# Up product of a decoder layer: some low parts by accumulating loads, convolutions in pieces, and the last product's sums reloaded pair by pair

## The chip, the cores and the metric

The kernel runs on one core of one Trainium2 chip. The metric is the device time of one execution in microseconds (us); the time shown for a kernel is the median of its runs. The profile names the engines PE (TensorE's matmuls), PEld (its weight loads), DVE (VectorE), ACT (ScalarE), POOL (GpSimd) and SP (SyncE); SP and POOL issue nearly all the DMAs.

## The reference

One decoder layer on x of 256 tokens by 2048, all in float32. A wide input product feeds forgetting attention (8 heads), a matrix memory (mLSTM, 4 heads) and two gates; the two branches are projected, gated, added, multiplied by w_out and added to x. Then comes the feed-forward part, where the change works:

```python
        h2 = rmsnorm(x, norm2_g[l])
        u = causal_dwconv(jnp.einsum('bsd,df->bsf', h2, w_up[l]), conv_w[l], conv_b[l])
        u_gate, u_val = u[..., :D_FF], u[..., D_FF:]
        x = x + jnp.einsum('bsf,fd->bsd', jax.nn.silu(u_gate) * u_val, w_down[l])
```

causal_dwconv adds three taps over the tokens to each channel; D_FF is 5632. So w_up is 2048 x 11264 and w_down 5632 x 2048.

## The kernel before

**Products in parts.** Every product is made of three matmuls in the type fp32r: each operand is split into a high part (a copy rounded to fp32r) and a low part (the operand minus its high part), and high x low, high x high and low x high are added in PSUM (`prod`, L287). Activations are split by `put` (L195). Weights are split as they arrive: ACT writes the high part wh, DVE subtracts it from the raw weights and writes the low part wl (`split_sub`, L172 and L173).

**Weights.** They are stored as chunks of 128 x 2048 floats (1 MB), each cut into pieces (`add_chunk`, L100). SP loads chunks into a ring of three buffers raw (L135 to L137); wh and wl have rings of three. `next_sub` (L178) asks for the chunks up to two ahead, splits the coming pieces, and hands out the next.

**Blocks of the large products.** `s_block` (L280) makes 256 tokens x 1024 columns in one go, over pairs of 128 rows of the weights. A pair of kind p ("plain") takes two pieces and 8 x 3 = 24 matmuls of 128 x 512. A pair of kind S saves one product in eight by working with sums and differences of the weights (DVE makes them, L157 to L167, tile sums) and of the activations (`put_sums`): four pieces, 21 matmuls, four more PSUM tiles, and some additions afterwards. Strings such as UP_PAIRS give the kinds: the up product has 8 pairs a block, 2 of them S, in 11 blocks (up0 to up10); the last product (y0, y1) has 22 pairs a block, 8 of them S, in two blocks.

**Work between the pieces.** `tasks` is a list of closures; each piece of an s_block takes the next `per_piece` of them (`run_tasks`, L190). During block b of the up product they are the transposes of block b-1's result (`as_columns`, L933: PE, then ACT), its convolutions (`convolved`, L944: ACT, DVE, ACT, DVE) and the split of the outcome g (tile ghl) with, for some pairs, its sums. All engines take their instructions in the order in which this Python code issues them, as the scheduler has placed them.

**Memory.** The tag a8 is a ring of 15 buffers of 8 KB per partition. g has 22 pairs. The first N_OUT = 6 are sent to DRAM (g_dram, L978) and come back (gback, L1010) before the last product; the sums of the 8 S pairs go to s_dram (L975) and come back in three loads of 1 MB (s_ops, L1016). POOL issues these DMAs, and in its order they stand one behind the other.

**Start.** x, transposed, is loaded by SP in eight parts between the first chunks of weights; POOL builds the constants (identity matrices, masks, sel) and then, on the same queue, issues the two loads of x as rows (xt, L486).

Of the kernel before, what the change touches and what calls it, by code (L numbers as in the profile page):

```python
# [10 lines left out]
F32 = mybir.dt.float32  # L11
# [6 lines left out]
P = 128  # L18
# [34 lines left out]
C_G1, C_G2, C_QG, C_KG, C_MG, C_CONV = 0, 16, 32, 33, 34, 42  # L53
CST = C_CONV + 2 * NF * 4


# [11 lines left out]
def trunk(ctx: ExitStack, tc: tile.TileContext, a):  # L68
# [16 lines left out]
    def a8(name, shape, dtype=F32):  # L85
        return big.tile([P, *shape], dtype, tag="a8", bufs=15, name=name)

# [25 lines left out]
    def add_pairs(ap, patterns):  # L113
        for i, kind in enumerate("".join(patterns)):
            pieces = ("b", "b21", "t13", "t24") if kind == "S" else ("whole", "whole")
            add_chunk(ap[i], 2048, pieces)

# [7 lines left out]

    raws, subs, s_tiles = {}, {}, {}
    n_chunk = len(chunks)
# [11 lines left out]
    def split_sub(j):  # L139
# [9 lines left out]

        if kind == "whole":  # L150
            src = raw[:, s * n : (s + 1) * n]
# [20 lines left out]
        nc.scalar.activation(wh[:, :n], src, AF.Copy)  # L172
        nc.vector.tensor_tensor(wl[:, :n], src, wh[:, :n].bitcast(F32), ALU.subtract)  # L173
        subs[j] = (wh[:, :n], wl[:, :n])

    state = {"sub": 0}

    def next_sub(ahead=2):  # L178
        j = state["sub"]
        state["sub"] = j + 1  # L180
        i = subs_of[j][0]
        for c in range(i, i + 3):
            load_chunk(c)
        for q in range(j, j + ahead):
            split_sub(q)
        return subs.pop(j)
# [3 lines left out]
    def run_tasks(n):  # L190
        for _ in range(min(n, len(tasks))):
            tasks.pop(0)()

# [86 lines left out]
    def s_block(name, pairs, s_ops, pattern, pools, dst, add=True, per_piece=0):  # L280
# [22 lines left out]
        for m, kind in enumerate(pattern):  # L303
# [3 lines left out]

            if kind == "p":
# [79 lines left out]
    for _ in range(9):  # L388
# [5 lines left out]
    ident = const.tile([P, P], F32, name="ident")  # L394
    make_identity(nc, ident)
    identb = const.tile([P, P], BF16, name="identb")
    make_identity(nc, identb)
    upper = const.tile([P, P], F32, name="upper")
    make_upper_triangular(nc, upper)
    ones = const.tile([P, P], F32, name="ones")  # L400
    nc.gpsimd.memset(ones, 1.0)
    mhalf = const.tile([P, 8], F32, name="mhalf")
    nc.gpsimd.memset(mhalf, -0.5)
    mask_qk = const.tile([P, P], BF16, name="mask_qk")
    make_causal_mask(nc, mask_qk, mask_val=-BIG)
    mask_st = const.tile([P, P], BF16, name="mask_st")
    nc.gpsimd.memset(mask_st, 0.0)
    nc.gpsimd.affine_select(
        out=mask_st, in_=mask_st, compare_op=ALU.is_ge, fill=BIG, base=0, pattern=[[1, P]],
        channel_multiplier=-1,  # L410
    )


    sel = const.tile([3 * 32, FH, P], BF16, name="sel")
    nc.gpsimd.memset(sel, 0.0)
    for i in range(3):
        nc.gpsimd.affine_select(
            out=sel, in_=sel, compare_op=ALU.not_equal, fill=1.0, base=-32 * i,
            pattern=[[-1, FH], [0, P]], channel_multiplier=1,
        )  # L420
    nFT = const.tile([3 * 32, S], BF16, name="nFT")
    MT = const.tile([3 * 32, S], BF16, name="MT")
    nc.gpsimd.memset(MT, 0.0)

# [53 lines left out]
    for k in range(KD):  # L478
# [4 lines left out]
        product_b(z, hT, k, [wh[:, c] for c in cols], [wl[:, c] for c in cols], k == 0, k == KD - 1)  # L483
        if k == 2:
            for tok in range(2):
                nc.gpsimd.dma_start(xt[tok], a["x"][tok * P : (tok + 1) * P, :])  # L486
        if k >= KD // 2:
# [73 lines left out]

    qT, kT, fv = a8("qT", [FH, S]), a8("kT", [FH, S]), a8("fv", [2, FOXW])
    mqkT = a8("mqkT", [2, MH, S])
# [10 lines left out]
    def qk_evac(z, dst, b, gcol, scale, name):  # L574
        for tok in range(2):
# [16 lines left out]
            def finish(tok=tok, qn=qn):  # L592
                ps = transpose4(qn, f"ps_{name}{b}{tok}")
                g = cst[:, gcol : gcol + 1]
                out = dst[:, 4 * b : 4 * b + 4, tok * P : (tok + 1) * P]
                nc.vector.tensor_scalar(out, ps, g, scale, ALU.mult, ALU.mult)
# [3 lines left out]
    for b in range(2):  # L600
        qk_evac(block_b(f"fq{b}", hT, KD, 512), qT, b, C_QG, FD**-0.5, "q")
    for b in range(2):
        qk_evac(block_b(f"fk{b}", hT, KD, 512), kT, b, C_KG, 1.0, "k")

# [39 lines left out]
    def fox0(h):  # L644
        ps = aux_tile(f"ps_s{h}")
        for q0, n, o in ((0, P, 0), (P, S, P)):
            out = ps[:, o : o + n]
            mm(out, qT[:, h, q0 : q0 + P], kT[:, h, :n], True, False)
            mm(out, sel[:, h, :], nFT[:, :n], False, False)
# [293 lines left out]

    def convolved(j):  # L944
        u, out = us.pop(j), []
        for i in range(2):
            f = 2 * j + i
            w = [cst[:, C_CONV + 4 * f + q : C_CONV + 4 * f + q + 1] for q in range(4)]
            t = scratch("t", [P, S], tag="u1k", bufs=5)
            nc.scalar.activation(t, u[:, i, :], AF.Identity, scale=w[2], bias=w[3])  # L950
            for q in (1, 0):
                d = 2 - q
                nc.vector.scalar_tensor_tensor(  # L953
                    out=t[:, d:], in0=u[:, i, : S - d], scalar=w[q], in1=t[:, d:], op0=ALU.mult,
                    op1=ALU.add,
                )
            out.append(t)
        sg = scratch("sg", [P, S], tag="u1k", bufs=5)
        nc.scalar.activation(sg, out[0], AF.Silu)
        m = j // 2  # L960
        if j % 2 == 0:
            gvs[m] = scratch("gv", [P, 512])
        gv = gvs[m]
        nc.vector.tensor_tensor(gv[:, (j % 2) * S : (j % 2 + 1) * S], sg, out[1], ALU.mult)  # L964
        if j % 2 == 0:
            return
        if m % 2 == 0:
# [13 lines left out]

    nop = [lambda: None]
    first_tasks = list(tasks)
    tasks.clear()
    tasks.extend(nop * 4 + first_tasks + [norm2])
    for b in range(NF // 4):
        pools = (aux_tile, acc_tile) if b % 2 == 0 else (acc_tile, aux_tile)
        c = a8(f"c{b}", [2, 1024])
        dst = lambda tok, h, c=c: c[:, tok, h * 512 : (h + 1) * 512]
        q = s_block(f"up{b}", h2_pairs, up_ops, UP_PAIRS, pools, dst, False, 2)  # L990
        run_tasks(len(tasks))
# [5 lines left out]
        ts, es = [  # L997
            [lambda j=j, f=f, c=c: f(j, c) if c is not None else f(j) for j in range(4 * b, 4 * b + 4)]
            for f, c in ((as_columns, c), (convolved, None))
        ]  # L1000
        tasks.extend(nop * 4 + [ts[0]] + nop + [ts[1], es[0], ts[2], ts[3]] + nop + [es[1]])
        tasks.extend(nop + [es[2]] + nop + [es[3]])
# [9 lines left out]
    blocks = []  # L1012

    def load_sums(i):
        t = a8(f"s_ops{i}", [16 * P], F32R)
        nc.gpsimd.dma_start(t, s_dram[:, i * 16 * P : (i + 1) * 16 * P])  # L1016
        blocks.extend(t[:, q * P : (q + 1) * P] for q in range(16))


    n_sums = N_S * 6 // 16  # L1020
    for i in range(n_sums - 1):
        load_sums(i)
    tasks.append(lambda: load_sums(n_sums - 1))
    s_pos = [pos for pos, kind in enumerate(Y_PAIRS) if kind == "S"]

    def sums_of(pos):
        g, i = g_pairs[Y_ORDER[pos]], 6 * s_pos.index(pos)
        return [(g[:, 0, 0, P:], g[:, 0, 1, P:])] + [
            (blocks[i + c], blocks[i + 3 + c]) for c in range(3)
        ]  # L1030

    y_pairs, y_ops = Lazy(lambda pos: g_pairs[Y_ORDER[pos]]), Lazy(sums_of)
    for b in range(2):
# [4 lines left out]
        dst = lambda tok, h, xr=xr: xr[:, tok, h * 512 : (h + 1) * 512]  # L1038
        q = s_block(f"y{b}", y_pairs, y_ops, Y_PAIRS, pools, dst, True, 2)
        for h in range(2):  # L1040
# [83 lines left out]
```

## Time and profile before

| | us |
|---|---|
| three runs: median (lowest to highest) | 1435.16 (1434.25 to 1435.97) |
| the profiled execution: its own time | 1436.96 |
| the profiled execution: span, first to last instruction | 1435.2 |
| of the span: up to the up product, 0 to 703 us: PE busy | 690.7 |
| of the span: about the up product, 703 to 1192 us: PE busy | 466.4 |
| of the span: last product, 1192 to 1436 us: PE busy | 235.0 |

The profile comes from one execution. Its page gives, for each engine, the busy time and the number of instructions; other views give the same by line, by form (operation with its shapes), by window of time, or in order of time, with the engine or DMA that ended each wait. A row "a<-b" names the tile that is written and those that are read; "x16" is a count; L172 is line 172 of the kernel. For a DMA the last number is the median time from its issue to its landing. Matmuls are pipelined, and their ends are modelled, so a PE that is busy is not always one that makes progress at its full pace; the distance between the starts of matmuls shows that.

### The profile page before, as it was taken

What the parts mean: (1) busy time and instruction counts of PE and PEld (TensorE: products, weight loads), DVE (VectorE), ACT (ScalarE), POOL (GpSimd) and SP (SyncE); (2) the same over time, 40 slices, a digit from 0 to 9 for tenths busy, and PEclk for the clock granted to TensorE, in tenths of its full rate; (3) what the DMA queues carried; (4) which work ended last, traced back from release to release, by engine and by line L of the source; (5) the groups of instructions that cost most, each with busy time, mean ns of one, the idle gap of its engine ahead of it and who ended that gap; (6) DMA issues with size and microseconds to landing.
All of it is one profiled execution on the core that took longest, in us unless ns stands there. A gap on an engine that the chain in (4) does not pass through costs nothing. (4 is left out here: it accounts for less than half of the span.)

```text
span 1435.2 us, 17408 instructions
## 1 busy us (share of the span) xinstructions
PE 1392.1 (97%) x6356; PEld 1139.1 (79%) x6356; DVE 1120.2 (78%) x1526; ACT 828.9 (58%) x1152; POOL 44.0 (3%) x81
## 2 busy tenths in 40 slices
PE   8999999999999999999999999999999999999998
PEld 7988888887878888877778777787777777778877
DVE  5555766557888767878888889888988897987786
ACT  6645554445656544566566666766676666563553
POOL 2001000000000000000000000000000010000000
PEclk8999999999999999999999999999999999999999
DMA  8645554443555565555565655464546567666553
GB/s 286 222 175 177 176 205 148 175 145 128 199 193 217 200 227 193 202 205 206 179 213 179 228 182 199 150 216 163 190 168 216 179 228 289 231 221 246 200 199 117
DMA packets 45654, 282.48 MB, mean 197 GB/s; under 512 B 5185, under 2 KB 7249, under 8 KB 14465
## 3 DMA queue, kind: packets, MB, share of 16 engines
q1 hardware_dynamic: 39168, 260.20, 51.4%
q0 software_dynamic: 6256, 21.16, 4.2%
q8 instruction: 49, 0.80, 0.2%
q14 instruction: 37, 0.30, 0.1%
q10 hardware_dynamic: 144, 0.02, 0.0%
HBM read 270.87 MB, written 10.49 MB: 196 GB/s over the span
## 5 line engine op out<-in xcount | busy, mean ns | idle before, releaser
L172 ACT ACTIVATE wh<-raw 128x1024 fp32r<-128x1024 f32 (+2 forms) x496 | 491.9, 999 | 402.5 <-PE p L233 47.1
L173 DVE TENSOR_TENSOR wl<-raw,wh 128x1024 fp32r<-128x1024 f32 (+2 forms) x496 | 563.5, 1150 | 186.5 <-ACT wh L172 183.7
L173 DVE TENSOR_TENSOR wl<-sums,wh 128x1024 fp32r<-128x1024 f32 x102 | 124.0, 1222 | 48.6 <-ACT wh L172 48.1
L172 ACT ACTIVATE wh<-sums 128x1024 fp32r<-128x1024 f32 x102 | 107.7, 1057 | 75.1 <-PE y1q L233 19.1
L953 DVE SCALAR_TENSOR_TENSOR t<-u,cst,t 128x255 f32<-128x255 f32 (+1 forms) x176 | 76.6, 480 | 4.4 <-ACT t L950 3.7
L233 PE MATMUL p<-wh,am 128*128 128x512 f32 x256 | 79.5, 391 | 0.0
L157 DVE TENSOR_TENSOR sums<-raw 128x1024 f32<-128x1024 f32 x51 | 62.4, 1224 | 5.8 <-DMA raw<-in_w_dn 3.4
L233 PEld LDWEIGHTS p<-wh,am 128*128 128x128 f32 x256 | 47.6, 188 | 9.7
L233 PE MATMUL y0q<-wh,ghl 128*128 128x512 f32 x172 | 52.6, 392 | 0.0
L233 PE MATMUL y1q<-wh,ghl 128*128 128x512 f32 x172 | 52.1, 390 | 0.0
L233 PE MATMUL p<-wl,am 128*128 128x512 f32 x128 | 49.9, 390 | 0.0
L950 ACT ACTIVATE t<-u,cst 128x256 f32<-128x256 f32 x88 | 48.3, 594 | 0.7
L233 PE MATMUL mog<-wh,hT 128*128 128x348 f32 (+1 forms) x192 | 43.9, 340 | 4.1 <-DVE hT L202 4.1
L996 ACT ACTIVATE c<-c,rho 128x512 f32<-128x512 f32 x44 | 31.6, 720 | 25.4 <-DVE c L995 25.4
L233 PE MATMUL g0q<-wh,hN 128*128 128x512 f32 x128 | 41.3, 401 | 0.0
L233 PE MATMUL mv<-wh,hT 128*128 128x512 f32 x128 | 40.3, 396 | 0.0
L233 PE MATMUL fq<-wh,hT 128*128 128x512 f32 x128 | 40.0, 394 | 0.0
L233 PE MATMUL fk<-wh,hT 128*128 128x512 f32 x128 | 39.8, 392 | 0.0
L233 PE MATMUL fv<-wh,hT 128*128 128x512 f32 x128 | 39.6, 391 | 0.0
L233 PEld LDWEIGHTS mog<-wh,hT 128*128 128x128 f32 x192 | 35.0, 203 | 5.3 <-ACT wh L172 3.1
L233 PEld LDWEIGHTS y1q<-wh,ghl 128*128 128x128 f32 x172 | 32.3, 188 | 6.9
L233 PEld LDWEIGHTS y0q<-wh,ghl 128*128 128x128 f32 x172 | 32.1, 188 | 6.7
(627 smaller groups left out, 3181.3 us busy)
## 6 DMA issues: line engine op xcount, KB each, us to landing
raw<-in_w_up SPq DMA_DIRECT2D x88, 1024.0 KB, 4.9
raw<-in_w_dn SPq DMA_DIRECT2D x44, 1024.0 KB, 4.9
raw<-in_w_g SPq DMA_DIRECT2D x32, 1024.0 KB, 4.9
raw<-in_w_fox SPq DMA_DIRECT2D x24, 1024.0 KB, 4.9
raw<-in_w_p SPq DMA_DIRECT2D x16, 1024.0 KB, 4.9
raw<-in_w_out SPq DMA_DIRECT2D x16, 1024.0 KB, 4.9
raw<-in_w_mqk SPq DMA_DIRECT2D x8, 1024.0 KB, 4.8
raw<-in_w_mv SPq DMA_DIRECT2D x8, 1024.0 KB, 4.9
```

The lines of the kernel that those rows point to most:

```text
L157: nc.vector.tensor_tensor(sums[:, :1024].rearrange("p (i c) -> p i c", i=2), raw[:, :512].unsqueeze(1).to_broadcast([P, 2, 512]), src.rear ...
L172: nc.scalar.activation(wh[:, :n], src, AF.Copy)
L173: nc.vector.tensor_tensor(wl[:, :n], src, wh[:, :n].bitcast(F32), ALU.subtract)
L233: nc.tensor.matmul(out, lhsT, rhs, start=start, stop=stop)
L950: nc.scalar.activation(t, u[:, i, :], AF.Identity, scale=w[2], bias=w[3])
L953: nc.vector.scalar_tensor_tensor(out=t[:, d:], in0=u[:, i, : S - d], scalar=w[q], in1=t[:, d:], op0=ALU.mult, op1=ALU.add,)
L996: nc.scalar.activation(v, v, AF.Copy, scale=rho[:, tok : tok + 1])
```

## The change

1. In the up product the kind of the plain pairs becomes d. Its first piece is split as before. For its second ("loaded") piece, ACT still writes wh, but the low part is no longer DVE's: `load_low` has ACT write the negated rounded weights into a buffer wd (a ring of two), and POOL issues a DMA that adds the weights from DRAM to what stands in wd. `next_sub` asks for this for up to eight pieces ahead, where the chunk is near enough.
2. `convolved` does half of one column block per call, `finished` does the split of g and its sums, and a table (`at_pieces`) gives the piece of the next block at which each call is made; one task list is taken per piece. The last block has a table of its own, as its convolutions run under y0.
3. The last product: N_OUT is 8; a8 has 14 buffers; the sums come back in eight loads of two S pairs (768 KB), four for each of the blocks y0 and y1, each asked for when the previous one comes into use; the S pairs stand one place later in Y_PAIRS.
4. kT moves into the two wd buffers (not yet in use then).
5. At the start the constants are built behind hT[8], and the loads of xt are written at k = 4 and k = 6.

```diff
-UP_PAIRS = "ppSpSppp"
-Y_PAIRS = "ppp" + "Sp" * 7 + "S" + "pppp"
+UP_PAIRS = "ddSdSddd"
+Y_PAIRS = "pppp" + "Sp" * 8 + "pp"
-N_OUT = 6
+N_OUT = 8
...
+PIECES = {"S": ("b", "b21", "t13", "t24"), "p": ("whole", "whole"), "d": ("whole", "loaded")}
...
-        return big.tile([P, *shape], dtype, tag="a8", bufs=15, name=name)
+        return big.tile([P, *shape], dtype, tag="a8", bufs=14, name=name)
...
+        nc.scalar.activation(wh[:, :n], src, AF.Copy)
+        if kind == "loaded":
+            subs[j] = (wh[:, :n], lows.pop(j))
+            return
         wl = wpool.tile([P, 1024], F32R, tag="wl", bufs=3, name=f"wl{j}")
-        nc.scalar.activation(wh[:, :n], src, AF.Copy)
         nc.vector.tensor_tensor(wl[:, :n], src, wh[:, :n].bitcast(F32), ALU.subtract)
...
+    def load_low(j):
+        if j >= len(subs_of) or j in lows or subs_of[j][2] != "loaded":
+            return
+        i, s, _ = subs_of[j]
+        load_chunk(i)
+        src, n = chunks[i][0], chunks[i][1] // 2
+        c = slice(s * n, (s + 1) * n)
+        lows[j] = wpool.tile([P, 1024], F32R, tag="wd", bufs=2, name=f"wd{j}")
+        nc.scalar.activation(lows[j], raws[i][:, c], AF.Copy, scale=-1.0)
+        nc.gpsimd.dma_start(lows[j], src[:, c], accum_op=ALU.add)
...
         for c in range(i, i + 3):
             load_chunk(c)
+        for q in range(j, j + 8):
+            if subs_of[min(q, len(subs_of) - 1)][0] <= i + 1:
+                load_low(q)
         for q in range(j, j + ahead):
             split_sub(q)
         return subs.pop(j)
...
-        if k == 2:
-            for tok in range(2):
-                nc.gpsimd.dma_start(xt[tok], a["x"][tok * P : (tok + 1) * P, :])
+        if k in (4, 6):
+            tok = k // 2 - 2
+            nc.gpsimd.dma_start(xt[tok], a["x"][tok * P : (tok + 1) * P, :])
+        if k == 7:
+            make_constants(hT[8][:, 1, :])
...
+        at_pieces({
+            2: [t[0]], 3: [t[1]], 8: [e[0][0]], 9: [e[0][1]], 14: [e[1][0]], 15: [e[1][1]],
+            16: [t[2], f[0]], 17: [t[3]], 18: [e[2][0]], 19: [e[2][1]], 21: [e[3][0]],
+            22: [e[3][1]], 23: [f[1]],
+        } if b < NF // 4 - 1 else {
+            1: [t[0]], 2: [t[1], e[0][0]], 3: [e[0][1]], 4: [t[2], e[1][0]], 5: [e[1][1]],
+            6: [t[3], e[2][0]], 7: [e[2][1]], 12: [e[3][0]], 13: [e[3][1], f[0]], 18: [f[1]],
+        })
...
+    def load_sums():
+        i = len(ring) % (N_S // 2) * 12 * P
+        if len(ring) < N_S:
+            ring.append(a8(f"s_ops{len(ring)}", [12 * P], F32R))
+            nc.gpsimd.dma_start(ring[-1], s_dram[:, i : i + 12 * P])
```

How the order of instructions moves is shown at the change from block up5 to block up6. On ACT, before (wh378 is the high part of piece 378, the first of block up6; c5 is the result of block up5, scaled here; u20 is its first transposed column block):

```order
L172 ACTIVATE wh377_7799<-raw163_7742 128x1024
L172 ACTIVATE wh378_7817<-raw164_7780 128x1024
L996 ACTIVATE c5_7456<-c5_7456,rho_4794 128x512 x2
L172 ACTIVATE wh379_7821<-raw164_7780 128x1024
L996 ACTIVATE c5_7456<-c5_7456,rho_4794 128x512
L172 ACTIVATE wh380_7864<-raw165_7815 128x1024
L996 ACTIVATE c5_7456<-c5_7456,rho_4794 128x512
L172 ACTIVATE wh381_7880<-raw165_7815 128x1024
L172 ACTIVATE wh382_7899<-raw166_7862 128x1024
```

On ACT at the same place with the change:

```order
L174 ACTIVATE wh379_7964<-raw164_7890 128x1024
L1035 ACTIVATE c5_7589<-c5_7589,rho_4796 128x512
L191 ACTIVATE wd379_7951<-raw164_7890 128x1024
L1035 ACTIVATE c5_7589<-c5_7589,rho_4796 128x512 x3
L191 ACTIVATE wd379_8011<-raw164_7890 128x1024
L174 ACTIVATE wh380_8017<-raw165_7946 128x1024
L174 ACTIVATE wh381_8033<-raw165_7946 128x1024
L191 ACTIVATE wd381_8014<-raw165_7946 128x1024
L174 ACTIVATE wh382_8059<-raw166_8009 128x1024
L191 ACTIVATE wd381_8055<-raw165_7946 128x1024
```

Two fills of wd stand for each loaded piece, 379 and 381, between the splits of the same pieces. The first fill of 379 waits for PE's last matmul with wd377, which lay in the same buffer, and the first fill of 381 for PE's last with wd379.

On POOL the same stretch with the change holds only these DMAs; before, POOL issues nothing there but the stores of g and of the sums of the block:

```order
L192 DMA wd377_7895<-in_w_up 128x1024
L192 DMA wd377_7948<-in_w_up 128x1024
L192 DMA wd379_7951<-in_w_up 128x1024
L192 DMA wd379_8011<-in_w_up 128x1024
L192 DMA wd381_8014<-in_w_up 128x1024
L192 DMA wd381_8055<-in_w_up 128x1024
L192 DMA wd387_8115<-in_w_up 128x1024
```

Each of them waits for its fill, and the fill of wd377_7895 itself waits until the second copy of piece 375 has landed in its buffer.

On PE the low parts of a loaded piece now stand behind both pieces' high parts (block up6, piece 379):

```order
L256 MATMUL up6q11_8008<-wl378_7956,h20_4789 128x512
L256 MATMUL up6q00_8005<-wh379_7964,h20_4789 128x512 x2
L256 MATMUL up6q10_8007<-wh379_7964,h20_4789 128x512 x2
L256 MATMUL up6q01_8006<-wh379_7964,h20_4789 128x512 x2
L256 MATMUL up6q11_8008<-wh379_7964,h20_4789 128x512 x2
L968 MATMUL ps_u20_8068<-ident_115,c5_7589 128x128 x4
L968 MATMUL ps_u21_8094<-ident_115,c5_7589 128x128
L256 MATMUL up6q00_8005<-wd379_7951,h20_4789 128x512
L256 MATMUL up6q10_8007<-wd379_7951,h20_4789 128x512
```

The copy that PE reads is the one with the lower number, wd379_7951; nothing reads wd379_8011. Of a block's six loaded pieces (in up6: 379, 381, 387, 393, 395 and 397) all are alike in this.

More of the change, by code (lines that the diff above doesn't have):

```diff
@@ L114, in add_pairs @@
         for i, kind in enumerate("".join(patterns)):
-            pieces = ("b", "b21", "t13", "t24") if kind == "S" else ("whole", "whole")
-            add_chunk(ap[i], 2048, pieces)
+            add_chunk(ap[i], 2048, PIECES[kind])
     for name in ("w_fox", "w_mqk", "w_mv"):
@@ L124, in trunk @@
     add_pairs(a["w_dn"], [Y_PAIRS] * 2)
-    raws, subs, s_tiles = {}, {}, {}
+    raws, subs, s_tiles, lows = {}, {}, {}, {}
     n_chunk = len(chunks)
@@ L191, in run_tasks @@
         for _ in range(min(n, len(tasks))):
-            tasks.pop(0)()
+            t = tasks.pop(0)
+            for f in t if isinstance(t, list) else [t]:
+                f()
     def put(hi, lo, src, scale=None):
@@ L394, in trunk, with make_constants @@
     ident = const.tile([P, P], F32, name="ident")
-    make_identity(nc, ident)
     identb = const.tile([P, P], BF16, name="identb")
-    make_identity(nc, identb)
     upper = const.tile([P, P], F32, name="upper")
-    make_upper_triangular(nc, upper)
     ones = const.tile([P, P], F32, name="ones")
-    nc.gpsimd.memset(ones, 1.0)
     mhalf = const.tile([P, 8], F32, name="mhalf")
-    nc.gpsimd.memset(mhalf, -0.5)
     mask_qk = const.tile([P, P], BF16, name="mask_qk")
-    make_causal_mask(nc, mask_qk, mask_val=-BIG)
     mask_st = const.tile([P, P], BF16, name="mask_st")
[L407 to L411, printed above, removed]
-    sel = const.tile([3 * 32, FH, P], BF16, name="sel")
[L415 to L420, printed above, removed]
+    sel = const.tile([3 * 32, FH, P], BF16, name="sel")
     nFT = const.tile([3 * 32, S], BF16, name="nFT")
     MT = const.tile([3 * 32, S], BF16, name="MT")
-    nc.gpsimd.memset(MT, 0.0)
+    def make_constants(after):
+        at = nc.gpsimd.tensor_copy(mhalf[:, :1], after[:, :1].bitcast(F32))
+        with tc.issue_after(at.ins):
+            nc.gpsimd.memset(mhalf, -0.5)
+            make_identity(nc, ident)
+            nc.gpsimd.memset(ones, 1.0)
+            make_upper_triangular(nc, upper)
+            make_identity(nc, identb)
+            make_causal_mask(nc, mask_qk, mask_val=-BIG)
+            nc.gpsimd.memset(mask_st, 0.0)
+            nc.gpsimd.affine_select(
+                out=mask_st, in_=mask_st, compare_op=ALU.is_ge, fill=BIG, base=0, pattern=[[1, P]],
+                channel_multiplier=-1,
+            )
+            nc.gpsimd.memset(MT, 0.0)
+            nc.gpsimd.memset(sel, 0.0)
+            for i in range(3):
+                nc.gpsimd.affine_select(
+                    out=sel, in_=sel, compare_op=ALU.not_equal, fill=1.0, base=-32 * i,
+                    pattern=[[-1, FH], [0, P]], channel_multiplier=1,
+                )
     def bf16_parts(parts, rest):
@@ L560, in trunk @@
     tasks.extend([gates_a, gates_b, gates_c])
-    qT, kT, fv = a8("qT", [FH, S]), a8("kT", [FH, S]), a8("fv", [2, FOXW])
+    qT, fv = a8("qT", [FH, S]), a8("fv", [2, FOXW])
+    kT = [wpool.tile([P, 4, S], F32, tag="wd", bufs=2, name=f"kT{b}") for b in range(2)]
     mqkT = a8("mqkT", [2, MH, S])
@@ L942, in as_columns, with convolved @@
         nc.scalar.activation(us[j].rearrange("p h s -> p (h s)"), ps, AF.Copy)
[L944 to L959, printed above, removed]
+    def convolved(j, i):
+        u = us[j]
+        f = 2 * j + i
+        w = [cst[:, C_CONV + 4 * f + q : C_CONV + 4 * f + q + 1] for q in range(4)]
+        t = scratch("t", [P, S], tag="u1k", bufs=5)
+        nc.scalar.activation(t, u[:, i, :], AF.Identity, scale=w[2], bias=w[3])
+        for q in (1, 0):
+            d = 2 - q
+            nc.vector.scalar_tensor_tensor(
+                out=t[:, d:], in0=u[:, i, : S - d], scalar=w[q], in1=t[:, d:], op0=ALU.mult,
+                op1=ALU.add,
+            )
+        if i == 0:
+            gvs["sg"] = scratch("sg", [P, S], tag="u1k", bufs=5)
+            nc.scalar.activation(gvs["sg"], t, AF.Silu)
+            return
+        sg = gvs.pop("sg")
+        del us[j]
         m = j // 2
@@ L996, in trunk @@
                 nc.scalar.activation(v, v, AF.Copy, scale=rho[:, tok : tok + 1])
[L997 to L1002 removed]
+        t, e = [lambda j=j, c=c: as_columns(j, c) for j in range(4 * b, 4 * b + 4)], [
+            [lambda j=j, i=i: convolved(j, i) for i in range(2)] for j in range(4 * b, 4 * b + 4)
+        ]
+        f = [lambda m=m: finished(m) for m in (2 * b, 2 * b + 1)]
+        at_pieces({
[6 more added lines that the diff above has]
+        })
+    s_pos = [pos for pos, kind in enumerate(Y_PAIRS) if kind == "S"]
+    ring = []
+    def load_sums():
[3 more added lines that the diff above has]
+            nc.gpsimd.dma_start(ring[-1], s_dram[:, i : i + 12 * P])
+    load_sums()
     for m in range(N_OUT):
@@ L1011, in trunk, with sums_of @@
         g_pairs[m] = t[:, m % 2].rearrange("p (k l s) -> p k l s", k=2, l=2)
[L1012 to L1032, printed above, removed]
+    def sums_of(b, pos):
+        g, (r, i) = g_pairs[Y_ORDER[pos]], divmod(s_pos.index(pos) + b * N_S, 2)
+        if i == 0:
+            load_sums()
+        at = [ring[r][:, q * P : (q + 1) * P] for q in range(6 * i, 6 * i + 6)]
+        return [(g[:, 0, 0, P:], g[:, 0, 1, P:])] + [(at[c], at[3 + c]) for c in range(3)]
+    y_pairs = Lazy(lambda pos: g_pairs[Y_ORDER[pos]])
     for b in range(2):
```

32 lines of the change are left out of this document (18 added, 14 removed).

## The prediction

> **What bounds the kernel now.** I read first the page's busy shares, then the windows, then PE's timeline over one block of the up product, then ACT and DVE by form over the same block.
>
> ```profile
> span 1435.2 us, 17408 instructions
> PE 1392.1 (97%) x6356; PEld 1139.1 (79%) x6356; DVE 1120.2 (78%) x1526; ACT 828.9 (58%) x1152; POOL 44.0 (3%) x81
> ```
> PE is busy 97% of the span, and the change leaves every matmul in place (6353 in both programs). So only waits can be won, 43 us at the very most, and only part of them lies in the stages that change.
>
> ```profile
> 811.40:857.90 46.50, 44.67 (x203) 36.23 (x202) 41.37 (x57) 31.21 (x44) 1.06 (x2) 1.00 0.59 204
> 764.91 0.61 PE L233 MATMUL up2q<-wh,h 128*128 128x512 f32 x2
> 765.59 0.61 PE L233 MATMUL up2q<-wh,h 128*128 128x512 f32 x2
> 770.36 0.60 PE L937 MATMUL ps_u<-ident,c 128*128 128x128 f32 x4
> 770.71 0.71 PE L233 MATMUL up2q<-wh,h 128*128 128x512 f32 x2
> 782.40 0.50 PE L233 MATMUL up2p<-wl,us 128*128 128x512 f32 x1 [0.28 <-DVE wl L173]
> 793.14 0.50 PE L233 MATMUL up2p<-wh,us 128*128 128x512 f32 x1 [1.55 <-ACT wh L172]
> 811.41 0.61 PE L233 MATMUL up3q<-wh,h 128*128 128x512 f32 x2
> ```
> The first row is one whole block of the up product (columns: window, length, busy PE, PEld, DVE, ACT, POOL, granted clock, DMA share, GB/s). A block starts at 764.91 and the next at 811.41: **46.5 us**. From 764.91 to 765.59 three matmuls pass, 0.227 us each; a block has 6 plain pairs of 24 and 2 S pairs of 21, 186 in all, 42.2 us. Four groups of four transposes cost some 0.4 us each (770.36 to 770.71, and a slower matmul behind), 1.6 us. So PE needs 43.8 us, and 2.7 us of each block are waits and their after-effects, 29.7 us in 11 blocks. They sit in the S pairs, where PE waits for a split weight (wh from ACT, wl from DVE).
>
> ```profile
> L172 ACT ACTIVATE wh<-raw 128x1024 fp32r<-128x1024 f32 x15 | 15.5, 1054 | 9.0 <-PE up3q L233 7.3 <-issue 1.4 <-PE up2q L233 0.4
> L173 DVE TENSOR_TENSOR wl<-raw,wh 128x1024 fp32r<-128x1024 f32 x14 | 16.9, 1222 | 3.8 <-ACT wh L172 3.8
> ```
> In that block DVE is busy 41.4 of 46.5 us and late in bursts, ACT 31.2.
>
> **The change part by part.** *Taken away:* per block 6 of DVE's wl, 6 x 1.22 = 7.3 us. With the convolutions in halves over fixed pieces, DVE's bursts get shorter. If nothing else came, the 2.7 us would largely go.
>
> *Added:* each low part is now an ACTIVATE of the negated high part into a buffer wd, and a POOL DMA that adds the weights to it. The order holds not 66 of each but **132**: load_low looks only whether the piece is in lows, and split_sub takes it out, so the next call builds it a second time. Of the 132 buffers PE reads 66. ACT gets 12 x 1.05 = 12.6 us per block: 31.2 + 12.6 = 43.8, all that PE's 43.8 us leave, on an engine that works in order. This has no cover: any wait at the head of ACT's queue is then passed on to PE.
>
> *The added wait.* There are two wd buffers. With the useless second copies, a useful copy mostly finds both taken: it goes into the buffer that PE has just read, or waits until a second copy's DMA has landed there. Through block up5 the buffers tie this chain: PE ends piece 357, fill 359, PE reads it (4 matmuls), fill 361, PE reads it (4), fill 367, PE runs from 367's first matmul to 373's last (55), the second copy of 375 is filled and lands, only then fill 377, PE reads it (7), and the next block starts the same way. That is five fills and 70 matmuls, 70 x 0.227 = 15.9 us. A fill is ACT's 1.05 us, the DMA from issue to landing (L), and about 0.4 us for three handovers between engines (estimate):
>
> block = 15.9 + 5 x (1.45 + L) = **23.1 + 5 L**, if over 43.8.
>
> Behind each waiting fill stand, on ACT, the wh of the next pieces, the scalings of c and the column copies, and PE waits for those too; on POOL the DMAs of the other copies and the stores of the sums.
>
> *How long is L?* No accumulating DMA is in the trace, so bounds come from POOL's DMAs beside the same stream of weights.
>
> ```profile
> g_dram<-ghl POOLq DMA_DIRECT2D x6, 512.0 KB, 3.0
> g_dram<-ghl POOLq DMA_DIRECT2D x2, 512.0 KB, 4.1
> gback<-g_dram POOLq DMA_DIRECT2D x1, 512.0 KB, 6.0
> s_ops<-s_dram POOLq DMA_DIRECT2D x1, 1024.0 KB, 7.6
> raw<-in_w_up SPq DMA_DIRECT2D x8, 1024.0 KB, 4.9
> ```
> These are 512 KB stores (all six; the two in this block), the one 512 KB load that was issued alone (about 1126 us), a single 1 MB load (about 1228 us) and the weights of this block. From below: 3.0 gives 38, so PE's 43.8 stands. From above: if an addition moves as much as 1 MB, 7.6 gives 61.1. An accumulating load is nearest to the 512 KB load, in size, direction, queue and neighbours: L = 6.0, block 53.1, **6.6 us more**. Break-even is 46.5, at L = 4.7. The Trainium skill ("DMA: Bandwidth & Descriptors", Anatomy of one DMA) has a POOL-issued DMA at 2.0 us plus its bytes over 436 GB/s, by my estimate 3.2 us for 512 KB; by that the chain hides and the change wins. The trace's 6.0 disagrees, since the weights move beside it.
>
> *Start.* The constants leave the first 10 us of POOL, and with them what slowed DVE there; but the two loads of x, which stood behind the constants on POOL's queue, now wait for nothing and go out some 6 us earlier, into the loads that PE starts on.
>
> ```profile
> 5.29 3.60 DVE L202 SCALAR_TENSOR_TENSOR hT<-xT,cst,hT 128x256 fp32r<-128x256 f32 x2 [4.15 <-ACT hT L201]
> 10.40 0.87 DVE L202 SCALAR_TENSOR_TENSOR hT<-xT,cst,hT 128x256 fp32r<-128x256 f32 x2
> 7.42 1.19 PE L233 MATMUL mog<-wh,hT 128*128 128x348 f32 x6 [2.21 <-DVE hT L202]
> 8.54 1.09 POOL L486 DMA_DIRECT2D xt<-in_x  x2
> 0.00:20.00 20.00, 14.80 (x57) 11.43 (x57) 9.84 (x13) 8.73 (x14) 9.34 (x27) 0.83 0.91 333
> ```
> Two hT took 3.60 us beside the constants, and 0.87 after: 2.7 us to win. The 2.1 MB of x at 333 GB/s are 6.3 us, to lose if all of it goes ahead of what PE needs. I take 0, bounds -3 and +6.
>
> *Last product.* Its sums come back in eight loads of two S pairs, a ring of two or three; two more pairs of g go through DRAM. A reload is asked for two S pairs (90 matmuls, 20 us) ahead, beside the 7.6 us for 1 MB: hidden; if it were not, eight times a few us.
>
> ```profile
> 1214.29 0.74 PE L233 MATMUL y0p<-wh,ghl 128*128 128x512 f32 x2 [1.06 <-ACT wh L172]
> 1215.78 0.50 PE L233 MATMUL y0p<-wl,ghl 128*128 128x512 f32 x1 [0.52 <-DVE wl L173]
> 1227.77 0.50 PE L233 MATMUL y0p<-wh,s_ops 128*128 128x512 f32 x1 [1.11 <-ACT wh L172]
> 1240.40 0.50 PE L233 MATMUL y0p<-wl,s_ops 128*128 128x512 f32 x1 [0.24 <-DVE wl L173]
> 1377.64 0.50 PE L233 MATMUL y1p<-wl,s_ops 128*128 128x512 f32 x1 [0.82 <-DVE wl L173]
> ```
> These waits are all that can be won there, 3.8 us; the first fall in the last convolutions, which now come earlier. I take -2, bounds -4 and +4.
>
> **The sum**, against the profiled execution's own 1436.96 us (1.8 us above the median of 1435.16): 11 x 6.6 = 73, 0 and -2 make **1508 us**.
>
> **The rivals.**
> *The fills are hidden (faster).* If L is below some 4 us, the chain is shorter than PE's work, DVE's relief shows, and a block takes 44 to 46: 11 x (-0.5 to -2.5), with -2 at the end some 1407 to 1429. For it speak the stores of 3.0 and 4.1 us; against it that an addition has to read its target as well, that the only lone load took 6.0, and that ACT has no time left.
> *Two reads per addition: the DMA engines become the bound.*
>
> ```profile
> q1 hardware_dynamic: 1152, 8.39, 51.5%
> q0 software_dynamic: 288, 1.05, 6.8%
> ```
> In the same block 8.39 MB of weights hold the 16 engines for 51.5% of 46.5 us, 24 us; that is 2.86 us per MB. Twelve additions are 6.29 MB; if each costs twice, 36 us. With the 3 us of the other DMAs a block takes 63, 16.5 more: 11 x 16.5 = 182, some 1616 us. If each costs once, 45 us, and the DMA engines are no bound beside the forecast's 53. The Trainium skill ("Collectives: The Full Stack", The bandwidth ceiling) says that a reduction in the DMA path runs at half a copy's rate, because it reads two sources. Nothing in this trace shows that yet.
> *No change.* L near 4.7, and what DVE and PE win is what ACT and the buffers take.
> *The change doesn't do what it says.* That part is sure, in that half of the additions serve nothing; it is in the sum.
>
> **How the numbers follow.** Forecast (slot chain, L from 4.8 to 7, 1443 to 1570): 0.50. Engines bound (above 1570): 0.20. Hidden (below 1433): 0.23. Within 0.2%, which is about what a measurement can tell from no change: 0.07. Faster 0.23, slower 0.70. The range leaves out the upper part of the engines' case and little at the bottom, where nothing better than 11 x 2.7 and both small gains, 1400, is to be had: 1410 to 1620.
>
> **What would show it.** Right: wd 132 times on ACT and on POOL; wd's DMAs at about 6 us to landing; up blocks of 51 to 57 us with PE waiting for DMA wd and for ACT wh, ACT near full; DVE's wl 430 times. Wrong: wd landing in under 4.5 us and blocks of 44 to 46 (hidden); raw landing late and a DMA share near 1 in every block (engines bound); or waits of PE in the last product for s_ops.

## The result, and the profile after

| | median, us | lowest to highest | ratio to before, 95% interval |
|---|---|---|---|
| before | 1434.7 | 1433.67 to 1435.97 | |
| with the change | 1699.86 | 1698.05 to 1707.96 | 1.1859 (1.1819 to 1.1898) |

The change makes the kernel 18.6% slower. The forecast, 1508 us, had the sign but not the size; the time also lies above the range.

The page of the changed kernel begins so (span; busy time, share and instructions of each engine):

```profile
span 1697.0 us, 17645 instructions
PE 1471.1 (87%) x6356; PEld 1183.2 (70%) x6356; DVE 1053.0 (62%) x1460; ACT 948.2 (56%) x1284; POOL 164.5 (10%) x223
```

PE has the same 6356 instructions and no longer fills the span. Where the time went shows a cut at the first matmul of block up0 and of block y0. The windows of before (columns: window, length, busy PE, PEld, DVE, ACT, POOL, granted clock, DMA share, GB/s), the up product and then y0:

```profile
669.00:1192.80 523.80, 500.79 (x2222) 404.06 (x2223) 459.15 (x650) 346.76 (x482) 16.65 (x31) 0.98 0.56 196
1192.80:1314.10 121.30, 118.37 (x522) 94.89 (x522) 102.31 (x123) 69.08 (x83) 1.64 (x3) 1.00 0.63 228
```

The same two stretches of the changed kernel, with the single block up6 between them:

```profile
672.90:1452.50 779.60, 578.97 (x2223) 447.64 (x2224) 390.13 (x578) 462.21 (x607) 127.97 (x161) 0.87 0.86 217
1098.50:1168.00 69.50, 50.41 (x203) 39.27 (x203) 35.38 (x50) 41.98 (x55) 10.22 (x12) 0.89 0.85 212
1452.50:1576.20 123.70, 119.07 (x522) 95.41 (x521) 104.35 (x129) 70.31 (x84) 4.26 (x8) 0.99 0.74 266
```

The up product took 523.8 us and now takes 779.6, **+255.8 of the span's +261.8**. The start gave +3.9 (up0 begins at 672.9, not 669.0), the last product +2.1 (244.5 behind 1452.5, against 242.4 behind 1192.8). A mean block is 70.9 us, and PE is busy in 52.6 of it.

Inside block up6, PE's timeline shows its waits (start, length, instruction, count, idle time before it and what ended it):

```profile
1105.84 1.20 PE L256 MATMUL up6q<-wd,h 128*128 128x512 f32 x4 [1.77 <-DMA wd<-in_w_up]
1115.51 1.67 PE L256 MATMUL up6q<-wd,h 128*128 128x512 f32 x4 [3.57 <-DMA wd<-in_w_up]
1126.83 1.22 PE L256 MATMUL up6p<-wh,us 128*128 128x512 f32 x2 [5.10 <-ACT wh L174]
1164.95 1.65 PE L256 MATMUL up6q<-wd,h 128*128 128x512 f32 x3 [6.96 <-DMA wd<-in_w_up]
1166.40 0.63 PE L256 MATMUL up6q<-wl,h 128*128 128x512 f32 x1
1166.83 1.05 PE L256 MATMUL up6q<-wh,h 128*128 128x512 f32 x2
1167.68 0.63 PE L256 MATMUL up6q<-wd,h 128*128 128x512 f32 x1
```

PE waits for additions to land, and for wh where ACT stands behind a fill. Over the whole up product the trace puts 149 us of PE's waits down to additions and 46 us to wh. ACT's fills of wd in the same block show both links (start, length, instruction, idle time before it and what ended it; rows between are left out):

```profile
1117.22 1.06 ACT L191 ACTIVATE wd<-raw 128x1024 fp32r<-128x1024 f32 x1 [0.20 <-PE up6q L256]
1124.77 1.06 ACT L191 ACTIVATE wd<-raw 128x1024 fp32r<-128x1024 f32 x1 [6.50 <-DMA wd<-in_w_up]
1125.73 1.04 ACT L174 ACTIVATE wh<-sums 128x1024 fp32r<-128x1024 f32 x1
1148.69 1.05 ACT L191 ACTIVATE wd<-raw 128x1024 fp32r<-128x1024 f32 x1
1157.91 1.06 ACT L191 ACTIVATE wd<-raw 128x1024 fp32r<-128x1024 f32 x1 [4.27 <-DMA wd<-in_w_up]
```

A fill waits 6.50 us for an earlier addition, and the wh behind it ends just before PE goes on at 1126.83. The wait is not the whole price: behind the wait of 6.96 us the matmuls pass 0.42 us apart (two from 1166.83 to 1167.68), not the 0.227 of before. Over the up product 200.6 us are idle (779.6 less 579.0 busy), and the matmuls' busy time has grown by 78.2 us.

The page's groups that answer to the forecast (busy time, mean ns of one, idle time before and what ended it):

```profile
L179 DVE TENSOR_TENSOR wl<-raw,wh 128x1024 fp32r<-128x1024 f32 (+3 forms) x430 | 483.9, 1139 | 306.8 <-ACT wh L174 305.1
L191 ACT ACTIVATE wd<-raw 128x1024 fp32r<-128x1024 f32 x132 | 139.0, 1053 | 270.2 <-DMA wd<-in_w_up 219.1
L192 POOL DMA_DIRECT2D wd<-in_w_up x132 | 112.7, 853 | 665.0 <-ACT wd L191 627.3
```

There are 132 fills and additions and 430 wl, and ACT waits 219 us at the head of its queue for earlier additions to land. The DMA view of the up product (queues: packets, MB, share of the 16 engines' time; issues: count, KB, median us to landing):

```profile
q0 software_dynamic: 22253, 76.74, 51.1%
q1 hardware_dynamic: 12631, 92.08, 34.6%
raw<-in_w_up SPq DMA_DIRECT2D x84, 1024.0 KB, 7.3
wd<-in_w_up POOLq DMA_DIRECT2D x129, 512.0 KB, 7.8
```

An addition lands after **7.8 us** (taken: 6.0), and the weights after 7.3 instead of 4.9.

### The profile page after: what moved, and what is told of

It is laid out like the page before. It is cut to its first block, busy times and chain, and to the rows that moved or that the text cites. A ratio compares the mean times of both kernels' runs of the same rounds, so it can differ in the third digit from the quotient of the medians.

```text
span 1697.0 us, 17645 instructions
## 1 busy us (share of the span) xinstructions
PE 1471.1 (87%) x6356; PEld 1183.2 (70%) x6356; DVE 1053.0 (62%) x1460; ACT 948.2 (56%) x1284; POOL 164.5 (10%) x223
## 5 line engine op out<-in xcount | busy, mean ns | idle before, releaser
L179 DVE TENSOR_TENSOR wl<-raw,wh 128x1024 fp32r<-128x1024 f32 (+3 forms) x430 | 483.9, 1139 | 306.8 <-ACT wh L174 305.1
L191 ACT ACTIVATE wd<-raw 128x1024 fp32r<-128x1024 f32 x132 | 139.0, 1053 | 270.2 <-DMA wd<-in_w_up 219.1
L192 POOL DMA_DIRECT2D wd<-in_w_up x132 | 112.7, 853 | 665.0 <-ACT wd L191 627.3
L983 DVE SCALAR_TENSOR_TENSOR t<-u,cst,t 128x255 f32<-128x255 f32 (+1 forms) x176 | 82.3, 479 | 43.0 <-ACT t L980 41.5
L256 PEld LDWEIGHTS p<-wh,am 128*128 128x128 f32 x256 | 47.6, 188 | 9.7
L256 PE MATMUL y0q<-wh,ghl 128*128 128x512 f32 x164 | 51.1, 397 | 0.0
L256 PE MATMUL up0q<-wh,h 128*128 128x512 f32 x104 | 35.7, 432 | 7.7 <-ACT hv L920 7.7
```

The lines of the kernel that those rows point to most:

```text
L191: nc.scalar.activation(lows[j], raws[i][:, c], AF.Copy, scale=-1.0)
L192: nc.gpsimd.dma_start(lows[j], src[:, c], accum_op=ALU.add)
L256: nc.tensor.matmul(out, lhsT, rhs, start=start, stop=stop)
L983: nc.vector.scalar_tensor_tensor(out=t[:, d:], in0=u[:, i, : S - d], scalar=w[q], in1=t[:, d:], op0=ALU.mult, op1=ALU.add,)
```

## The experiments

Two causes are to be told apart. *Slot chain*: two wd buffers, half of their turns spent on copies that nobody reads, tie each block to five landings in a row. *DMA engines*: an addition costs them twice a copy, so that the weights and 132 additions no longer fit. A third, *ACT's load*, is checked on the way. Each ratio is to runs of the kernel before on the same chip (medians 1433.74 to 1434.67).

### The rest of the change alone: e2_plain

```diff
-UP_PAIRS = "ddSdSddd"
+UP_PAIRS = "ppSpSppp"
```

> The changed kernel with the pairs of the up product plain again (no accumulating loads at all); the start, the convolutions in pieces and the reload ring of the last product stay. If the whole loss comes from the low parts, as every theory has it, this is at or below the kernel before: blocks of 44 to 46.5 us, 1405 to 1437. If the convolutions handed out in pieces or the reloads cost time of their own, it is above 1440.

Measured: **1402.96 us, ratio 0.9783 (0.9764 to 0.9801)**. Its windows of the up product and y0:

```profile
665.30:1154.30 489.00, 488.99 (x2223) 398.17 (x2224) 455.75 (x647) 343.15 (x480) 17.72 (x33) 1.00 0.61 209
1154.30:1279.10 124.80, 118.81 (x522) 94.72 (x521) 103.96 (x127) 70.22 (x84) 4.27 (x8) 1.00 0.71 254
```

The up product falls to 489.0 us, blocks to 44.5, and PE is busy in all of it. So the low parts cost 297 us, the rest of the change wins 32, and behind the convolutions in pieces PE waits for nothing here that the additions could have taken away.

### Each low part once: e1_once

```diff
-        if j >= len(subs_of) or j in lows or subs_of[j][2] != "loaded":
+        if j >= len(subs_of) or j in lows or j in subs or subs_of[j][2] != "loaded":
```

> The changed kernel, with load_low also leaving out pieces that are already split, so that each low part is built once: 66 additions, not 132. Both copies that go are read by nobody, so the output stays. Slot chain (two buffers, half of them held by useless copies, set the block of 70 us): the two buffers now simply alternate, a buffer's cycle is fill 1.05 + landing + 12 matmuls (2.7 us) against the 36 matmuls or 8.2 us that PE has in between, so at a landing of 5 to 6 us it hides and a block takes 44 to 48 us, the kernel 1405 to 1450. DMA engines (additions at twice a copy's engine time are the bound): 24 us of weights + 18 us of additions + 3 us others = 45 us per block, a DMA share near 0.95, late weights, a block of 47 to 52, the kernel 1440 to 1500. ACT's load: ACT falls by 6.3 us a block to about 37 us, a block falls by about that, 64 us, the kernel about 1630.

Measured: 1454.13 us, ratio 1.0145 (1.0116 to 1.0173). Windows, and the DMA view of the up product:

```profile
667.70:1207.70 540.00, 508.23 (x2222) 404.53 (x2223) 389.05 (x578) 400.45 (x540) 73.35 (x97) 0.97 0.88 254
```

```profile
q1 hardware_dynamic: 12562, 91.41, 45.6%
q0 software_dynamic: 13616, 45.35, 41.8%
raw<-in_w_up SPq DMA_DIRECT2D x84, 1024.0 KB, 7.1
wd<-in_w_up POOLq DMA_DIRECT2D x64, 512.0 KB, 7.1
```

The useless second copies were worth 246 of the 297 us. The other 51 stay, though: the time lies in the range of the DMA engines, not of the slot chain, and the engines are busy 0.88 of a phase in which only half of the additions run.

### The second copy filled but not sent: e4_fill_only

```diff
-        nc.gpsimd.dma_start(lows[j], src[:, c], accum_op=ALU.add)
+        if j not in subs:
+            nc.gpsimd.dma_start(lows[j], src[:, c], accum_op=ALU.add)
```

> The changed kernel, where the second, useless copy of each low part is only filled by ACT and not sent to the DMA (66 additions, 132 fills); output unchanged. Slot chain: a useless copy now holds its buffer only for its own fill, so blocks are near those of the kernel with each low part built once, plus what ACT's 6 useless fills cost: 45 to 52 us, 1420 to 1500. DMA engines: as with each low part built once, 1440 to 1500. ACT's load: nothing is won, since ACT's work is the same, 1680 to 1700.

Measured: 1472.41 us, ratio 1.0264 (1.0233 to 1.0294). ACT's 66 useless fills, with the turns of the buffers that they take, cost 18 us beside the run above; the 66 useless DMAs cost the other 227. ACT's load is not the cause. Slot chain and DMA engines are not told apart by this run: it lies in both ranges.

### Copies in place of additions: e3_copy and e5_once_copy

```diff
-        nc.gpsimd.dma_start(lows[j], src[:, c], accum_op=ALU.add)
+        nc.gpsimd.dma_start(lows[j], src[:, c])
```

The second of the two builds each low part once as well.

> The changed kernel with the accumulation taken off its 132 loads: they are plain 512 KB copies of the weights into the same buffers, so the low parts of these pieces hold the weights themselves and the output is not the reference's. Buffers, fills, issues and order stay. Slot chain: a block follows the landing time; with 6 us instead of 7.1 to 7.8 it falls by 5 x 1 to 2 us, to 60 to 66 us, the kernel 1580 to 1650, and PE still waits for wd. DMA engines: 132 x 512 KB at the weights' 2.87 us per MB are 18 us of a block instead of 35, the bound falls below PE's work and the kernel to 1435 to 1480. If accumulating costs no more than copying: 1690 to 1710.

> Each low part built once (66 loads) and the accumulation taken off, so these low parts hold the weights themselves and the output is not the reference's. It closes the square: 132 additions 1697, 132 copies 1577, 66 additions 1454. If the 51 us that 66 additions cost over plain pairs (1403) come from the engine time of adding, this is at 1403 to 1415, with blocks of 44.4. If they come from the two buffers, the fills or the order on ACT, which all stay, it is at 1435 to 1455.

Measured: 1576.61 us, ratio 1.0992 (1.0968 to 1.1017), and 1418.72 us, ratio 0.9897 (0.9882 to 0.9912). Both lie outside the ranges: 132 copies just below that of the slot chain (from 1580) and far above that of the DMA engines (to 1480), 66 copies between the two (to 1415, from 1435), nearer to that of the adding. For 132 copies, the window of the up product, the queue in it, and the page's landing time:

```profile
665.30:1325.40 660.10, 540.37 (x2222) 418.50 (x2223) 389.48 (x578) 459.75 (x607) 85.71 (x161) 0.94 0.76 256
```

```profile
q0 software_dynamic: 22206, 76.59, 36.2%
```

```profile
wd<-in_w_up POOLq DMA_DIRECT2D x132, 512.0 KB, 5.6
```

132 copies of the same bytes take 36.2% of 660.1 us, 239 us, where 132 additions took 51.1% of 779.6, 398. The same view of the run with plain pairs leaves 9.85 MB on that queue:

```profile
q0 software_dynamic: 3841, 9.85, 6.1%
q1 hardware_dynamic: 12645, 92.12, 54.2%
```

That is 6.1% of 489.0, 30 us. Without it a copy costs (239 - 30) / 66.7 MB = 3.1 us of the 16 engines per MB and an **addition (398 - 30) / 66.9 MB = 5.5**; the weights cost 54.2% of 489.0 over 92.1 MB, 2.9. The Trainium skill ("Collectives: The Full Stack", The bandwidth ceiling) says of collectives that a ReduceScatter runs at half the rate of an AllGather, which only copies, since its add reads two sources. This trace's plain accumulating load is close to that, 5.5 against 3.1 and 2.9.

The square is now closed: 132 additions 1700, 132 copies 1577, 66 additions 1454, 66 copies 1419, none 1403. Of the 51 us of 66 additions some 35 are the adding itself, 16 the copies, fills and buffers.

The slot chain shows too. From additions to copies the landing falls by 2.2 us (7.8 to 5.6) and a mean block by 10.9 (779.6 / 11 = 70.9 to 660.1 / 11 = 60.0): 5.0 us of block per us of landing (5.5 by the median of 5.8 within the up product), about the factor of the forecast's 23.1 + 5 L (23.1 is short by 8.8 and 8.9 us). That it comes out so near is partly luck: of the 10.9 us, 7.4 are idle time of PE and 3.5 are matmuls that run faster again, which the forecast's factor doesn't hold; and the copies take load off the DMA engines as well.

### A third wd buffer: e6_three and its control e7_two_wl2

```diff
-wl = wpool.tile([P, 1024], F32R, tag="wl", bufs=3, name=f"wl{j}")
+wl = wpool.tile([P, 1024], F32R, tag="wl", bufs=2, name=f"wl{j}")
...
-lows[j] = wpool.tile([P, 1024], F32R, tag="wd", bufs=2, name=f"wd{j}")
+lows[j] = wpool.tile([P, 1024], F32R, tag="wd", bufs=3, name=f"wd{j}")
```

kT, which stands in the same ring, gets the third buffer too. The control has the first of the two edits alone.

> The changed kernel with 132 additions and three wd buffers in place of two; one wl buffer is given up for the room (two in place of three), output unchanged. To be compared with the same without the third wd buffer. Slot chain: a third buffer takes most of the waits for a taken buffer away, blocks fall from 71 to 50 to 60, the time to 1480 to 1590. DMA engines (share 0.86 already): the third buffer only lets additions queue, landing grows from 7.8 to 10 us or more, the time stays within 40 us of its control.

> The control: the changed kernel with two wl buffers in place of three, and nothing else; output unchanged. 1690 to 1730 by every theory, since DVE has six low parts less in each block and PE waits for wd.

Measured: 1601.15 us, ratio 1.1166 (1.1132 to 1.1199), against the control's 1713.44, ratio 1.1947 (1.1918 to 1.1976). The window, and the landing times, of three buffers:

```profile
678.50:1349.10 670.60, 559.93 (x2223) 430.51 (x2224) 390.83 (x580) 455.78 (x606) 126.95 (x160) 0.91 0.97 253
```

```profile
raw<-in_w_up SPq DMA_DIRECT2D x84, 1024.0 KB, 8.9
wd<-in_w_up POOLq DMA_DIRECT2D x128, 512.0 KB, 9.0
```

Neither theory has it to itself, and the time lies in neither range. The third buffer takes 112 us away (1713.44 less 1601.15), so the buffers did tie the blocks; but it stops at 61.0 us a block with the DMA engines at **0.97**. That is about the block of the forecast's second rival, 63. With the engines as good as always busy, a fourth buffer should bring little more; no run shows it.

### Three buffers and each low part once: e10_once_three

> Each low part built once (66 additions) and three wd buffers, with two wl buffers in place of three; output unchanged. The open question is what the 51 us of 66 additions with two buffers (1454 against 1403) are. Buffers: a third one hides landings of 7 us, the kernel falls to 1403 to 1425. DMA engines (share 0.88 with two buffers): it stays at 1440 to 1460, or only a few us below.

Measured: 1451.25 us, ratio 1.0124 (1.0096 to 1.0152): the interval overlaps that of two buffers (1.0116 to 1.0173). With 66 additions the third buffer wins nothing that shows in the time. One thing is open: the wl buffer given up for it may cost something (14 us with 132 additions, 1713.44 less 1699.86), and no run has that alone with 66. PE's waits for wd do fall, from 30 to 11 us, but its busy time grows by 5.4 us (513.6 less 508.2). The window and the landing times:

```profile
674.60:1211.60 537.00, 513.58 (x2223) 404.25 (x2224) 390.74 (x586) 404.55 (x543) 73.36 (x97) 0.97 0.88 256
```

```profile
raw<-in_w_up SPq DMA_DIRECT2D x84, 1024.0 KB, 7.1
wd<-in_w_up POOLq DMA_DIRECT2D x64, 512.0 KB, 7.6
```

Weights land after 7.1 us as with two buffers, against 5.0 with plain pairs.

### Additions that nobody reads: e8_traffic and e9_traffic_in_step

```diff
-            subs[j] = (wh[:, :n], lows.pop(j))
-            return
+            lows.pop(j)
...
-        lows[j] = wpool.tile([P, 1024], F32R, tag="wd", bufs=2, name=f"wd{j}")
-        nc.scalar.activation(lows[j], raws[i][:, c], AF.Copy, scale=-1.0)
...
+        lows[j] = s_tiles["spare"].pop(0)
+        s_tiles["spare"].append(lows[j])
```

The second adds, ahead of the addition, a column that ACT makes from raw and POOL copies into the buffer.

> 132 additions whose result nobody reads: they go in turn onto two buffers filled once, without ACT's fills, while all low parts come from DVE as in plain pairs; PE, ACT and DVE have the work of the kernel with plain pairs (1403), and only POOL waits for an addition. Output unchanged. DMA engines as the bound: 24 us of weights and 35 us of additions do not go into 44.4 us, raw lands late, PE waits for it, blocks of 58 to 65, the kernel 1560 to 1640. Slot chain: traffic alone costs little, the additions run as fast as two in flight can and fall behind or keep up, blocks of 44 to 50, the kernel 1403 to 1465.

> The run with unread additions again, now held in step with the up product: before each of the 132 additions POOL copies one column that ACT has made from the arrived weights (0.2 us of ACT), so no addition can run ahead into earlier stages. PE reads none of them, all low parts come from DVE, output unchanged. If the slowdown needs only the traffic (weights land late because additions hold the DMA engines), up blocks are 55 to 62 us, the kernel 1520 to 1600. If it needs PE or ACT to wait for an addition, weights still land in time (7 to 9 us, three buffers of 5.5 us of work each), blocks are 44 to 48 us, the additions fall behind instead, the kernel 1403 to 1450.

The lines left out make the two buffers that the additions take in turn. The first run missed its aim. It measured 1657.5 us, ratio 1.1568 (1.1548 to 1.1587), but with nothing to hold them the additions ran from 237.5 to 838.2 us, in stages ahead of the up product, and there POOL's other work stood behind them:

```profile
L197 POOL DMA_DIRECT2D wd<-in_w_up x132: 866/866/941, 237.5 to 838.2; - x132
```

The up product, free of them, took 488.7 us. It says only what a queue full of slow DMAs does to whatever stands behind it.

The second measured 1585.38 us, ratio 1.1036 (1.0981 to 1.1092). The window and the DMA view of its up product, and what DVE waited for longest:

```profile
668.40:1317.30 648.90, 538.88 (x2222) 418.41 (x2223) 454.59 (x645) 352.08 (x604) 177.90 (x267) 0.91 0.96 252
```

```profile
q0 software_dynamic: 20773, 71.70, 57.2%
q1 hardware_dynamic: 12532, 91.26, 38.3%
raw<-in_w_up SPq DMA_DIRECT2D x84, 1024.0 KB, 8.1
wd<-in_w_up POOLq DMA_DIRECT2D x122, 512.0 KB, 8.5
```

```profile
DVE u L332 <- DMA s_dram<-se: 68.1, 4, 31.6
```

The time lies in the range of the traffic. PE read no addition, and yet a block took 59.0 us; 122 of the 132 were even issued in the phase, at a DMA share of 0.96. The two queues held the engines for 57.2% + 38.3% of 648.9 us, 620 us: 56 a block, more than PE's 44.5. That the traffic does not fit is shown. How PE came to wait is not cleanly the late weights, which land after 8.1 us: the stores of the sums stood behind the additions in POOL's queue (the DVE row, 68.1 us), and PE behind those. Of some 115 us of PE's waits the trace puts 39 down to that path and 70 to wl and wh, which are made from the weights.

### Which part wins: e11_old_last and e12_pieces_only

```diff
-N_OUT = 8
+N_OUT = 6
-Y_PAIRS = "pppp" + "Sp" * 8 + "pp"
+Y_PAIRS = "ppp" + "Sp" * 7 + "S" + "pppp"
...
+    load_sums(0)
+    tasks[5] = tasks[5] + [lambda: load_sums(1)]
+    tasks.append(lambda: load_sums(2))
```

Both have plain pairs and before's last product; e12_pieces_only has before's start as well.

> Plain pairs, the new start and the convolutions in pieces, but the last product as before: six pairs of g through DRAM, three S pairs' worth of sums less in the ring (three loads of 1 MB, the second and third of them issued from the first pieces of the last product, since the sums of one pair are stored only then), 15 large buffers. Output unchanged. By the phases of the traces the new last product costs 4 us (246.4 against 242.4), so this gives 1397 to 1401 where the new last product gave 1403. If the 4 us come from the convolutions that reach into the last product, it stays at 1401 to 1405.

> The same with the old start too: of the whole change only the convolutions handed out piece by piece are left. Output unchanged. By the phases of the traces these are worth 35 us in the up product (489.0 against 523.8) and the start 4 us (665.3 against 669.0): 1400 to 1406, and at least 3 us above the run with the new start. If the 35 us come from elsewhere, it is above 1415.

Measured: 1396.65 us, ratio 0.9742 (0.9728 to 0.9755), and 1397.15 us, ratio 0.9746 (0.9733 to 0.9760). These beat both kernels. The new start is worth nothing that can be measured (at least 3 us were expected); the convolutions in pieces are worth 37 us. Windows of e12_pieces_only, the up product and y0:

```profile
665.50:1155.10 489.60, 489.56 (x2222) 397.88 (x2223) 455.23 (x645) 344.68 (x480) 15.06 (x28) 1.00 0.61 212
1155.10:1272.70 117.60, 117.60 (x522) 94.92 (x521) 104.09 (x129) 69.53 (x85) 3.24 (x6) 1.00 0.64 228
```

y0 takes 117.6 us where the new last product takes 124.8 in the run with plain pairs. There, the waits of the new one in y0 (engine, line and what it waited for: us, times, longest):

```profile
PE y0p L256 <- DVE wl L179: 5.1, 4, 1.6
DVE sums L160 <- DMA raw<-in_w_dn: 7.4, 5, 2.2
```

PE waits for DVE, and DVE for weights that come late. The DMA view of y0, with the new last product and (second) with the old:

```profile
q0 software_dynamic: 2047, 7.98, 19.0%
raw<-in_w_dn SPq DMA_DIRECT2D x22, 1024.0 KB, 6.2
```

```profile
q0 software_dynamic: 864, 2.88, 7.4%
raw<-in_w_dn SPq DMA_DIRECT2D x22, 1024.0 KB, 4.9
```

POOL's queue moves 7.98 MB against 2.88, and the weights land after 6.2 us, not 4.9. The new last product costs some 6 us (1402.96 less 1396.65). Five reloads of sums of 768 KB are 3.9 of the 7.98 MB; most of the rest is g, of which seven loads land in y0 here and none with the old last product. What each of the two costs wasn't told apart.

### The runs side by side

| run | us | additions or copies | up product, us (from its profile) |
|---|---|---|---|
| before | 1434.7 | none | 523.8 |
| with the change | 1699.86 | 132 additions | 779.6 |
| control, two wl | 1713.44 | 132 additions | 791.4 |
| three buffers | 1601.15 | 132 additions | 670.6 |
| 132 copies | 1576.61 | 132 copies | 660.1 |
| unread, in step | 1585.38 | 132 additions | 648.9 |
| unread, run ahead | 1657.5 | 132 additions (before it) | 488.7 |
| second copy filled only | 1472.41 | 66 additions | 553.8 |
| each once | 1454.13 | 66 additions | 540.0 |
| each once, three buffers | 1451.25 | 66 additions | 537.0 |
| 66 copies | 1418.72 | 66 copies | 507.4 |
| plain pairs | 1402.96 | none | 489.0 |
| pieces alone | 1397.15 | none | 489.6 |
| pieces and new start | 1396.65 | none | 491.1 |

## Why the prediction was right or wrong

**Right in kind.** Each low part is built twice; PE waits for wd and, behind ACT's fills, for wh; with two buffers a block follows five landings, the 5 of 23.1 + 5 L. Block up6 has this chain link by link: landings of 5.6, 7.0, 9.4, 7.9 and 5.7 us, 35.5 in all. The 0.4 us for three handovers, for which the prediction shows no row, is borne out there: 0.29 us from a fill's end to POOL's DMA, and under 0.1 for the other two together. But ACT is not near full, though the forecast had it so: it is busy 462.2 of 779.6 us, since the blocks grew past it.

**Wrong in size, at the step "How long is L?".** L was taken from a plain 512 KB load, 6.0 us. For a plain load that is about right: 132 copies in the place of the additions land after 5.6. An addition lands after 7.8, and it takes 5.5 us of engine time per MB where a copy takes 3.1. The adding is what L left out: 5 x 1.8 x 11 = 99 us. By the estimate from the page that the prediction cited beside it (the Trainium skill, "DMA: Bandwidth & Descriptors", Anatomy of one DMA) L would have been 3.2 us; that is further off.

**The constant was short by 8.8 us a block, 97 us.** Two terms of it failed. It priced 70 matmuls at the pace of a PE that never stops; after a wait they go up to 0.42 us apart. And it put ACT's queue at nothing, though the prediction itself says that the wh of the next pieces stand there behind each waiting fill. In block up6 the chain's 70 matmuls take 18.9 us, not 15.9, 3.0 more; and ACT's queue costs some 8.0. The third landing is at 1127.9, but PE has waited for wh until 1126.83 and reads that low part only at 1132.84, 4.9 us late; and the buffer of the fill at 1148.69 was free at 1145.6, 3.1 us before ACT came to it. That makes 11 us over the constant in this block, where the mean is 8.8; for the other blocks the split wasn't worked out.

**The block of before was taken from a good one.** 46.5 us from one block; the mean is 523.8 / 11 = 47.6. The forecast added its 6.6 a block to a phase that was 12 us longer than it assumed, which takes 12 off the miss. With +4 at the start (taken: 0) and +2 in the last product (taken: -2), 99 + 97 - 12 + 8 = 192 us: that is the miss, 1700 less 1508.

**The rivals were taken as exclusive.** "Two reads per addition" had 0.20, with a block of 63 and 1616 us. Its price was about right (5.5 us per MB, 61.0 us with three buffers at a share of 0.97). But a dear addition also lands late, and so lengthens the slot chain, which with two buffers holds a block at 70.9 us while the engines are busy for 0.86 of it. The upper end was drawn at the second rival alone.

**What was won was missed.** The forecast put DVE's relief and the convolutions in pieces together as a gain of at most 29.7 us and then let ACT take it back. It is 35 us (523.8 to 489.0), it comes from the pieces without any low part by DMA, and it leaves PE without waits. "Hidden" (0.23) was never near: even 66 copies cost 16 us over plain pairs.

**Start and last product.** The start at 0 held within the scatter: up0 begins at 672.9 here, but at 665.3 with plain pairs and the same new start, and at 665.5 in the run with the old one. The last product was taken at -2 with a bound of +4, and "hidden" was right for s_ops: no wait of PE there is for them. But w_down lands later beside what POOL reloads, which wasn't in the sum; the new last product is some 6 us dearer than before's in the same kernel.

## What to carry to other kernels

A DMA that adds is not a free engine: price it by the engine time of the DMA queues per MB, beside the traffic that is already there, before its latency. Where a look-ahead builds something into a small ring, count the built ones in the order of instructions; a test that looks only into the table from which the user removes entries builds it again. And before work is moved to another engine, spread the bursts on the one that is late: here that alone took all waits out of the up product.

## What the runs showed that was not expected

- An accumulating DMA held the 16 engines for 5.5 us per MB, a copy of the same bytes on the same queue for 3.1; it landed after 7.8 us instead of 5.6.
- With PE's waits came slower matmuls. In the up product plain pairs have 489.0 us of busy PE and no wait; with the change 200.6 us of idle time go with 90.0 us more of busy time, with 132 copies 119.7 with 51.4, with 66 additions 31.8 with 19.2, at granted clocks of 0.87, 0.94 and 0.97. That is 0.4 to 0.6 us of slower matmuls to each us of wait; with 66 additions and three buffers it is 1.1 (23.4 with 24.6), so the ratio is no constant.
- DMAs with no order to hold them run ahead: 132 unread additions began at 237.5 us, 428 us before the up product starts with plain pairs (665.3). They held up what stood behind them, and in that run the up product began only at 920.4.
